# The first block of x and weights in two transfers, with roundings and products of 256 columns

## The chip, the cores and the metric

One core of one Trainium2 chip runs the whole kernel. The metric is device time in microseconds (us) of one execution; smaller is better. Before the change three runs took 620.62, 620.65 and 620.73 us (median 620.65). Beside these stands one profiled execution, with its trace.

## What is computed

A decoder trunk of two layers on 256 tokens with 1024 features, in float32. Each layer normalizes x, multiplies it by a wide input matrix (2848 columns), runs two kinds of attention on the parts, mixes them with an output matrix, and adds a squared-ReLU MLP. The part that matters here is the first product of the first layer:

```python
for l in range(DEPTH):
    h = _rms_norm(x, g_pre_mix[l])
    parts = jnp.split(h @ w_in[l], split_at, axis=-1)
    nq, kc, vc, ksel, vsel, kwin, vwin, gates, fq, fk, fv, ff = parts
    ...
    x = x + _rms_norm(mix, g_post_mix[l])
    h = _rms_norm(x, g_pre_mlp[l])
    y = jnp.square(jax.nn.relu(h @ w_up[l])) @ w_down[l]
    x = x + _rms_norm(y, g_post_mlp[l])
```

The kernel multiplies x by the gain of the norm first and scales the rows of the product by the inverse root mean square when it leaves PSUM, so the products need not wait for the norm.

## The kernel before

**Numbers.** PE multiplies in a rounded 32-bit form (`F32R`). To keep float32's accuracy every operand is split in a high half, the rounded value, and a low half, what rounding left over, and a product becomes three: high by high, high by low, low by high. `mm3` (lines 670 to 674) issues these three. So for each weight tile `wraw` there is a rounding to `whi` and a subtraction to `wlo`; for x there are `xT` high and low.

**Tiling.** Tokens are two tiles `t` of 128. The contraction over 1024 features is eight blocks `k` of 128. The input matrix is cut into column chunks (`CHUNKS`); the first that is worked on is chunk 0 of 512 columns here, in eight parts, one for each `k` (`FIRSTS`), then chunk 1 of 288 columns in four parts, and so on. `in_chunk` (lines 1060 to 1097) takes the parts in order and for each `k` and `t` calls `piece`, which issues the three products into the PSUM tile of `t`: six products of 512 columns for each `k` of chunk 0.

**The opening.** The host lays x transposed and the weights of chunk 0 side by side in one tensor, `first`: for each `k`, 256 columns of x and 512 of weights (`NFIRST` = 768), with eight columns of the gain ahead of block 0. Lines 611 to 625 load each block by one transfer on SP's queue: block 0 of 776 columns (388 KB), the others of 768. `first_xT` (lines 788 to 794) makes the two halves of x for a block, the high one on ACT and the low one on DVE, and copies the gain for block 0. `Weights.get` (lines 494 to 517) makes the two halves of a weight part: for the first two parts both on DVE, for later ones the rounding is on ACT and the subtraction on DVE. While the first block is on its way, PE runs five products of zeros (`WARM`, lines 639 to 642).

**What sets the order.** The kernel records every operation and a planner (`Recorder`, lines 184 to 408) decides the order on each engine from estimated costs, data dependencies, free buffers and due times; line 411 issues the result, so nearly all rows of the profile carry L411 and one goes by the tiles' names. `nc.after` names an operation that those recorded after it must not be planned ahead of; before the change it is set after the eighth block's transfer, and the tiles of x for the norm and the first constants follow it. Transfers take eight completion semaphores in turn, so the ninth transfer is issued only when the first has landed, the tenth when the second has, and so on.

Of the kernel before, what the change touches and what calls it, by code (L numbers as in the profile page):

```python
# [18 lines left out]
F32 = mybir.dt.float32  # L19
F32R = mybir.dt.float32r  # L20
AF = mybir.ActivationFunctionType
# [3 lines left out]
P = 128  # L25
D = 1024
S = 256
NT = 2
# [19 lines left out]
NFIRST = 768  # L48
# [433 lines left out]
class Weights:  # L482
# [11 lines left out]
    def get(self, i):  # L494
        nc, marks = self.nc, self.marks
        assert len(marks) == i
        marks.append(len(nc.ops))
        if i not in self.raw:
            nc.key = marks[max(i - LOAD_LEAD, 0)]
            self.load(i)  # L500
        kind, shape, src = self.units[i]
        raw = self.raw.pop(i)
        nc.key = None
        if kind == "raw":
            return raw
        nc.key = marks[max(i - SPLIT_LEAD, 0)]
        hi = self.tile([P] + shape, F32R, name="whi", tag="whi", bufs=WBUFS)
        lo = self.tile([P] + shape, F32R, name="wlo", tag="wlo", bufs=WBUFS)
        for j in range(shape[0]) if i < len(FIRSTS) else [slice(None)]:
            if i > 1:  # L510
                nc.scalar.activation(hi[:, j], raw[:, j], AF.Copy)
            else:

                nc.vector.tensor_copy(hi[:, j], raw[:, j])
            nc.vector.tensor_sub(lo[:, j], raw[:, j], hi[:, j].bitcast(F32))
        nc.key = None
        return hi, lo


def body(tc, A, consts_in, out):  # L520
    with ExitStack() as ctx:

        sb = {False: ctx.enter_context(tc.tile_pool(name="ops", bufs=1))}
        sb[True] = ctx.enter_context(tc.tile_pool(name="sb", bufs=1))
        pp = ctx.enter_context(tc.tile_pool(name="pp", bufs=1, space=PSUM))
        dram = ctx.enter_context(tc.tile_pool(name="dram", bufs=1, space=bass.MemoryType.DRAM))
        tc.nc.scalar.preload_act_table_set("natural_log_exp_and_others")
        rec = Recorder(tc.nc, tc)
        trunk(rec, A, consts_in, out, sb, pp, dram)
        rec.emit()  # L530


def trunk(nc, A, consts_in, out, sbp, pp, dram):
    def tile(shape, dtype, name, tag=None, bufs=1):
        return nc.tile(sbp[(tag or name) not in OPERANDS], shape, dtype, name, tag, bufs)

    def psum(tag):
        return nc.tile(pp, [P, 512], F32, tag, tag, {"acc": 2, "x": 2, "s": 3, "o": 1}[tag], psum=True)
# [20 lines left out]
    for l in range(DEPTH):  # L559
        at = 0  # L560
        for c, (a, b) in enumerate(CHUNKS):
# [3 lines left out]
            for q, (k0, k1) in enumerate(parts_of(l, c)):  # L565
# [4 lines left out]
                if (c, q) in RIDES:  # L570
                    s, j = RIDES[c, q]
# [24 lines left out]
    def weight(*key):  # L596
        return W.get(index[key])
# [13 lines left out]
    for k in range(8):  # L611
        if k in (2, 3):
            f = both[:, k - 2]
        elif k < 2:
            f = tile([P, D], F32, name="first", tag="raw", bufs=RBUFS)
        else:
            f = tile([P, D], F32, name="first", tag=f"act{k % 2}", bufs=2)
        o = 0 if k else 8
        f = f[:, 0:o + NFIRST]
        a = 8 + k * NFIRST - o  # L620
        nc.sync.dma_start(f, A["first"][:, a:a + o + NFIRST])
        if k == 0:
            gcol0 = f[:, 0:8]
        xTk.append(f[:, o:o + S])
        W.raw[k] = f[:, None, o + S:o + NFIRST]
# [14 lines left out]
    ps = psum("o")  # L640
# [29 lines left out]
    def mm3(ps, a, b, start, stop, check=True):  # L670

        for j, (u, v) in enumerate(((0, 0), (0, 1), (1, 0))):
            nc.tensor.matmul(ps, a[u], b[v], start=start and j == 0, stop=stop and j == 2,
                             skip_group_check=not check)
# [29 lines left out]
    def new_xT():  # L704
        both = tile([P, 8, 2, S], F32R, name="xT", bufs=1)
        return [both[:, :, j, :] for j in range(2)] + [both]
# [79 lines left out]
    xT = new_xT()  # L786
# [13 lines left out]
    for l in range(DEPTH):  # L800
        first = l == 0
# [105 lines left out]
        def hidden_part(s, q):  # L907
            if q == 0:
                T["w1"] = []
            T["w1"].append(weight(l, "w1" + s, q))  # L910
            if q == 3:
                T["hid"] = psum("o")
                with nc.stretch():
                    for i in range(16):
                        c = i % 4
                        nc.tensor.matmul(T["hid"][32 * c:32 * c + 32, :256],
                                         kst[s][:, i, :, :].rearrange("p g n -> p (g n)"), T["w1"][i // 4][:, c, :],
                                         start=i < 4, stop=i >= 12, tile_position=(0, 32 * c))
                    if s == "v":
                        compressed_scores()  # L920
                T["hs" + s] = tile([P, 256], F32, name="hs")
                nc.vector.tensor_copy(T["hs" + s], T["hid"][:, :256])
# [137 lines left out]
        def in_chunk(c, evac, by_token=False):  # L1060
            n = CHUNKS[c][1] - CHUNKS[c][0]
            parts = parts_of(l, c)
            begin = len(nc.ops)
            ps = [None, None]
            ws = {}

            def piece(t, k, hi, lo, k0):
                if k == 0:
                    ps[t] = psum("o" if by_token and t == 0 else "x" if c in (0, 2) else "acc")
                mm3(ps[t][:, :n], [y[:, k, t * P:t * P + P] for y in xT[:2]], (hi[:, k - k0, :], lo[:, k - k0, :]),  # L1070
                    k == 0, k == 7)

            if by_token:
                for t in range(NT):
                    for q, (k0, k1) in enumerate(parts):
                        if t == 0:
                            ws[q] = weight(l, "in", c, q)
                        for k in range(k0, k1):
                            piece(t, k, *ws[q], k0)
                            yield  # L1080
                    evac(t, ps[t])
                    yield
                return
            for q, (k0, k1) in enumerate(parts):
                w = weight(l, "in", c, q)
                for k in range(k0, k1):
                    for t in range(NT):
                        piece(t, k, *w, k0)
                        yield
                if (c, q) in RIDES:  # L1090
                    hidden_part(*RIDES[c, q])
                    yield
            nc.key = begin if EVKEY else None
            for t in range(NT):
                evac(t, ps[t])
            nc.key = None
            yield
# [78 lines left out]
        def stream():  # L1176
            def part(name, gen):
                yield from gen
                done.add(name)
            yield from part("c1", in_chunk(1, evac1))  # L1180
            yield from part("c2", in_chunk(2, evac2))
            yield from part("c3", in_chunk_T(3, "fqT"))
            yield from part("c4", in_chunk_T(4, "fkT"))
            yield from part("c5", in_chunk(5, evac5))
            for k in range(LASTK):
                while ("o", k) not in done or "nsa" not in done:
                    yield "wait"
                yield from part(("out", k), out_k(k))
# [187 lines left out]
        o = None  # L1376
        nc.lane = len(nc.ops)
        for i in range(len(flat) + 4):
# [16 lines left out]
            j = i - 3  # L1395
            if 0 <= j < len(flat) and flat[j][2] == 1 and flat[j][3] != 1:
                kind, pair, par, br = flat[j]
                if pair % 2:
                    o = psum("o")
# [3 lines left out]
                    cols = lambda q: [(q // 2) * HD] * 2 if br else [2 * q * HD, 2 * q * HD + HD]  # L1403
# [12 lines left out]
        xT = new_xT()  # L1416
# [108 lines left out]
        for fc in range(8):  # L1525
# [12 lines left out]
            if fc < 7:  # L1538
                for k in range(4):
                    w = weight(l, "dn", fc, k)  # L1540
# [6 lines left out]
            if not last_l:  # L1547
                xT = new_xT()
# [67 lines left out]
```

## Time and profile before

| | |
|---|---|
| median of 3 runs | 620.65 us (620.62 to 620.73) |
| the profiled execution's own time | 620.53 us |
| its span, first to last instruction | 618.4 us |
| PE busy | 611.0 us (99%) |
| DVE busy | 465.3 us (75%) |
| ACT busy | 388.9 us (63%) |
| moved by DMA | 118.86 MB, mean 192 GB/s |

PE is TensorE's matmul stream and PEld its loads of weights, which overlap the matmuls; DVE is VectorE, ACT ScalarE, SP the engine whose queue issues the transfers. A row of the timeline has its start in us from the span's start, its length in us (of all instructions merged in it), the engine, the line, the operation, what it writes and reads, its form, how many are merged, and in brackets how long the engine was idle before it and what ended that. The length of a matmul in the trace holds its whole passage through the array, so matmuls that follow each other overlap and the distance of their starts is what one costs. In a table of windows the columns are the window, its length, the busy time (and number of instructions) of PE, PEld, DVE, ACT and POOL, the granted clock of PE, the share of time that the DMA engines were busy, and GB/s.

### The profile page before, as it was taken

Reading aid. Unit: us, or ns where it says so; the run is one execution under the profiler, and the core shown is the slowest. Engines: PE = TensorE matmul, PEld = TensorE weight load, DVE = VectorE, ACT = ScalarE, POOL = GpSimd, SP = SyncE. Lnnn points to the kernel's source line nnn. Section 1 sums busy time; section 2 is a strip of 40 time slices with the busy share of each in tenths; the row PEclk is TensorE's granted clock in tenths of the full one; section 3 lists DMA queues with packets and bytes.
Section 4 is the critical chain, followed back from the end, with each engine's and each line's share of the span. In section 5 each row is a group of like instructions: output and inputs, shape, how many; then the busy total and the mean of one; then the engine's idle time right before and its main releaser. Section 6 shows DMA issues by size and latency. Waiting matters only on the chain.

```text
span 618.4 us, 9854 instructions
## 1 busy us (share of the span) xinstructions
PE 611.0 (99%) x3494; PEld 514.6 (83%) x3494; DVE 465.3 (75%) x1021; ACT 388.9 (63%) x760; POOL 10.8 (2%) x20
## 2 busy tenths in 40 slices
PE   9999999999999999999999999999999999999995
PEld 7989987788888888888888888778888888888884
DVE  6889998689966567557598999886996575566534
ACT  7766788567655555545466769775776456456522
POOL 0001200000000000000000020000000000000000
PEclk9999999999999999999999999999999999999998
DMA  8996746519765565564346781653386665666001
GB/s 323 401 355 209 268 137 223 171 36 307 254 191 191 182 205 196 184 197 140 107 137 239 265 312 71 204 205 104 131 299 203 191 197 175 200 197 181 32 0 68
DMA packets 34817, 118.86 MB, mean 192 GB/s; under 512 B 4144, under 2 KB 4304, under 8 KB 34768
## 3 DMA queue, kind: packets, MB, share of 16 engines
q1 hardware_dynamic: 34768, 118.23, 57.5%
q8 instruction: 27, 0.44, 0.3%
q14 instruction: 22, 0.18, 0.1%
HBM read 117.15 MB, written 1.07 MB: 191 GB/s over the span
## 4 chain that ended last, share of the span: by engine, by line
PE 99%; DVE 0%; DVEq 0%; issue 0%; ACT 0%
PE s L411 35%; PE acc L411 31%; PE x L411 25%; PE o L411 7%; DVE x L411 0%; DVE m L411 0%; DVEq L1612 0%; DVE rsqrt L411 0%; ACT rl L411 0%
## 5 line engine op out<-in xcount | busy, mean ns | idle before, releaser
L411 DVE TENSOR_TENSOR wlo<-wraw,whi 128x1024 fp32r<-128x1024 f32 (+1 forms) x188 | 225.5, 1201 | 97.9 <-ACT whi L411 57.9
L411 ACT ACTIVATE whi<-wraw 128x1024 fp32r<-128x1024 f32 (+1 forms) x188 | 195.4, 1042 | 108.2 <-PE acc L411 72.9
L411 PE MATMUL s<-xT,whi 128*128 128x512 f32 x448 | 106.5, 390 | 0.0
L411 PEld LDWEIGHTS s<-xT,whi 128*128 128x128 f32 x448 | 83.4, 188 | 16.8
L411 PE MATMUL x<-whi,aT 128*128 128x512 f32 x256 | 88.6, 391 | 0.0
L411 PE MATMUL acc<-whi,aT 128*128 128x512 f32 x256 | 88.4, 390 | 0.0
L411 PEld LDWEIGHTS s<-xT,wlo 128*128 128x128 f32 x448 | 57.4, 191 | 2.2
L411 PE MATMUL s<-xT,wlo 128*128 128x256 f32 x448 | 58.1, 283 | 0.0
L411 PEld LDWEIGHTS acc<-whi,aT 128*128 128x128 f32 x256 | 48.0, 188 | 10.0
L411 PEld LDWEIGHTS x<-whi,aT 128*128 128x128 f32 x256 | 48.1, 188 | 9.6
L411 PE MATMUL x<-wlo,aT 128*128 128x512 f32 x128 | 50.0, 390 | 0.0
L411 PE MATMUL acc<-wlo,aT 128*128 128x512 f32 x128 | 49.9, 390 | 0.0
L411 ACT ACTIVATE pr<-pr,st 128x256 f32<-128x256 f32 (+1 forms) x96 | 42.8, 449 | 5.8 <-DVE st L411 5.5
L411 PE MATMUL acc<-xT,whi 128*128 128x256 f32 (+1 forms) x192 | 42.4, 324 | 0.0
L411 PE MATMUL acc<-whi,xT 128*128 128x512 f32 (+1 forms) x128 | 37.2, 354 | 0.0
L411 PE MATMUL x<-whi,xT 128*128 128x512 f32 x112 | 35.7, 395 | 0.1
L411 PEld LDWEIGHTS acc<-xT,whi 128*128 128x128 f32 x192 | 31.7, 190 | 3.3 <-issue 0.8
L411 ACT ACTIVATE h<-s 128x256 f32<-128x256 f32 x56 | 21.2, 378 | 16.0 <-PE s L411 16.0
L411 ACT ACTIVATE rl<-h 128x512 f32<-128x512 f32 x28 | 17.7, 633 | 18.0 <-DVE h L411 18.0
L411 PE MATMUL acc<-xT,wlo 128*128 128x256 f32 x128 | 28.6, 286 | 0.0
L411 ACT ACTIVATE rl<-x 128x512 f32<-128x512 f32 x24 | 14.6, 610 | 22.2 <-PE x L411 18.0
L411 PEld LDWEIGHTS acc<-wlo,aT 128*128 128x128 f32 x128 | 24.0, 188 | 5.0
(220 smaller groups left out, 963.6 us busy)
## 6 DMA issues: line engine op xcount, KB each, us to landing
wraw<-in_w_up_dram SPq DMA_DIRECT2D x64, 512.0 KB, 4.0
wraw<-in_w_down_dram SPq DMA_DIRECT2D x64, 512.0 KB, 3.7
wraw<-in_w_in_dram SPq DMA_DIRECT2D x36, 512.0 KB, 4.9
wraw<-in_w_out_dram SPq DMA_DIRECT2D x16, 512.0 KB, 5.6
w<-in_cmp_w_k_dram SPq DMA_DIRECT2D x8, 512.0 KB, 4.9
w<-in_cmp_w_v_dram SPq DMA_DIRECT2D x8, 512.0 KB, 4.6
bias<-sums SPq DMA_DIRECT2D x8, 384.0 KB, 6.1
first<-in_first_dram SPq DMA_DIRECT2D x7, 384.0 KB, 5.2
```

The source lines that it names most:

```text
L411: getattr(getattr(self.nc, op.engine), name)(*[real(v) for v in args], **{k: real(v) for k, v in kw.items()})
```

## The change

Three edits belong together.

- Block 0 is loaded by two transfers: the gain, x and the first 256 columns of weights (520 columns), then the other 256 columns of weights. `nc.after` is set after the second of them, so that the seven other blocks stay behind both.
- Part 0 of the weights is rounded and subtracted in two halves of 256 columns, each on DVE.
- In `in_chunk`, block 0 of the first layer's chunk 0 is multiplied by column halves: both token tiles for the first 256 columns, then both for the rest, twelve products of 256 columns for six of 512. Only the first of them opens the PSUM tile's accumulation (`start`), and the group check is off, as a tile is now opened once for two column ranges.

```diff
@@ Weights.get
         for j in range(shape[0]) if i < len(FIRSTS) else [slice(None)]:
-            if i > 1:
-                nc.scalar.activation(hi[:, j], raw[:, j], AF.Copy)
-            else:
-
-                nc.vector.tensor_copy(hi[:, j], raw[:, j])
-            nc.vector.tensor_sub(lo[:, j], raw[:, j], hi[:, j].bitcast(F32))
+            for n in (slice(0, 256), slice(256, 512)) if i == 0 else [slice(None)]:
+                x, y, z = ((w[:, j, n] if i == 0 else w[:, j]) for w in (raw, hi, lo))
+                if i > 1:
+                    nc.scalar.activation(y, x, AF.Copy)
+                else:
+
+                    nc.vector.tensor_copy(y, x)
+                nc.vector.tensor_sub(z, x, y.bitcast(F32))
@@ trunk, the loads of the first blocks
-        nc.sync.dma_start(f, A["first"][:, a:a + o + NFIRST])
+        cut = o + NFIRST - 256 if k == 0 else o + NFIRST
+        for u, v in ((0, cut), (cut, o + NFIRST)):
+            if u < v:
+                nc.sync.dma_start(f[:, u:v], A["first"][:, a + u:a + v])
+        if k == 0:
+            nc.after = nc.ops[-1]
@@ in_chunk
-            def piece(t, k, hi, lo, k0):
-                if k == 0:
+            def piece(t, k, hi, lo, k0, n=slice(0, n)):
+                if k == 0 and not n.start:
                     ps[t] = psum("o" if by_token and t == 0 else "x" if c in (0, 2) else "acc")
-                mm3(ps[t][:, :n], [y[:, k, t * P:t * P + P] for y in xT[:2]], (hi[:, k - k0, :], lo[:, k - k0, :]),
-                    k == 0, k == 7)
+                mm3(ps[t][:, n], [y[:, k, t * P:t * P + P] for y in xT[:2]], (hi[:, k - k0, n], lo[:, k - k0, n]),
+                    k == 0 and not n.start, k == 7, check=False)
...
                 for k in range(k0, k1):
-                    for t in range(NT):
-                        piece(t, k, *w, k0)
-                        yield
+
+                    for cols in (slice(0, 256), slice(256, 512)) if first and c == 0 and k == 0 else [slice(0, n)]:
+                        for t in range(NT):
+                            piece(t, k, *w, k0, cols)
+                            yield
```

As the planner works on the whole program, its order moves elsewhere too: on PE some groups of products and transposes in the first layer's first three chunks change places, on SP one weight part of chunk 1 now comes ahead of the tiles of x, and ACT and DVE take the roundings and norm steps of chunk 1 in another order.

## The prediction

> **What bounds the kernel now.** I read the page first, for the span and the chain that ended last; then that chain in order of time for the opening; then the opening's timeline; then the queue of SP.
>
> ```profile
> span 618.4 us, 9854 instructions
> ...
> PE 99%; DVE 0%; DVEq 0%; issue 0%; ACT 0%
> ```
>
> PE is nearly the whole chain, so an edit pays only where it lets PE start sooner or removes a gap in its stream. The changed block is the first real work of PE:
>
> ```profile
> 4.66 0.05 issue
> 4.71 7.46 PE x L411 x30
> ```
>
> Thirty products run in these 7.46 us. What is their pace where nothing waits? Two starts of the same kind, three products apart:
>
> ```profile
> 10.43 0.62 PE L411 MATMUL x<-whi,xT 128*128 128x512 f32 x2
> ...
> 11.11 0.62 PE L411 MATMUL x<-whi,xT 128*128 128x512 f32 x2
> ```
>
> 0.68 us for three is 0.227 each. The last of the thirty starts at 4.71 + 7.46 - 0.39 = 11.78; 29 intervals took 7.07 us, where 29 x 0.227 = 6.58 would do: 0.49 us lost inside. Before them PE is idle too: the last warming product starts at 4.38 and the one before it at 4.27, so PE is free at about 4.49, 0.22 us before the first product.
>
> ```profile
> 4.27 0.39 PE L411 MATMUL o<-const-float32-0.0 128*128 128x128 f32 x2
> ...
> 4.38 0.27 PE L411 MATMUL o<-const-float32-0.0 128*128 128x128 f32 x1
> ```
>
> So 0.49 + 0.22 = 0.71 us, 0.11% of the time, is all that this part can give; 0.2% (1.24 us) is about what a measurement tells from no change. The timeline shows who makes PE wait:
>
> ```profile
> 4.14 0.43 DVE L411 CAST whi<-first 128x512 fp32r<-128x512 f32 x1 [2.97 <-DMA first<-in_first_dram]
> 4.14 0.51 ACT L411 ACTIVATE xT<-first 128x256 fp32r<-128x256 f32 x1 [2.12 <-DMA first<-in_first_dram]
> 4.48 0.16 DVE L411 COPY gcol<-first 128x8 f32<-128x8 f32 x1
> 4.60 0.69 DVE L411 TENSOR_TENSOR wlo<-first,whi 128x512 fp32r<-128x512 f32 x1
> 4.70 0.30 PEld L411 LDWEIGHTS x<-whi,xT 128*128 128x128 f32 x2 [0.23 <-ACT xT L411]
> ...
> 5.21 0.48 DVE L411 SCALAR_TENSOR_TENSOR xT<-first,xT 128x256 fp32r<-128x256 f32 x1
> 5.34 0.30 PEld L411 LDWEIGHTS x<-wlo,xT 128*128 128x128 f32 x2 [0.35 <-DVE wlo L411]
> ...
> 5.70 0.43 DVE L411 CAST whi<-first 128x512 fp32r<-128x512 f32 x1
> ...
> 5.76 0.51 ACT L411 ACTIVATE xT<-first,gcol 128x256 fp32r<-128x256 f32 x1 [1.11 <-DVE xT L411]
> 5.91 1.14 PE L411 MATMUL x<-whi,xT 128*128 128x512 f32 x4
> 6.16 0.69 DVE L411 TENSOR_TENSOR wlo<-first,whi 128x512 fp32r<-128x512 f32 x1
> 6.32 0.30 PEld L411 LDWEIGHTS x<-whi,xT 128*128 128x128 f32 x2 [0.22 <-ACT xT L411]
> ...
> 6.90 0.30 PEld L411 LDWEIGHTS x<-wlo,xT 128*128 128x128 f32 x2 [0.28 <-DVE wlo L411]
> ```
>
> Block 0 lands at 4.14, and ACT and DVE start at once. Block 1's work starts at 5.70 on DVE and 5.76 on ACT. Both are put down to DVE, which ends block 0 at 5.69; SP's queue tells another reason for the same instant:
>
> ```profile
> 0.74 3.95 SPq L411 DMA_DIRECT2D first<-in_first_dram  x8
> 4.73 0.54 SPq L411 DMA_DIRECT2D x<-in_x_dram  x1
> 5.69 0.33 SPq L411 DMA_DIRECT2D wraw<-in_w_in_dram  x1
> 6.64 0.33 SPq L411 DMA_DIRECT2D x<-in_x_dram  x1
> ...
> SPq L411 <- DMA first<-in_first_dram: 4.2, 7, 0.7
> ```
>
> Eight issues go out one behind the other; from then on each waits for a block to land, the tenth for block 1. So block 1 landed at about 5.67, and block 2 at 6.62: even if DVE were done with block 0 earlier, block 1 would not be there. This decides my forecast.
>
> **The change part by part.** *The first piece's landing.* It leaves out 128 KB of 388. At the rate of the full stream (399 GB/s below) that is 0.33 us, at the mean rate until block 0 landed (188) 0.70; the issue-to-landing latency may also not shrink at all.
>
> ```profile
> 0.74:4.12 3.38, 3.35 (x8) 2.75 (x9) 0.37 (x3) 1.27 (x1) 0.00 (x0) 1.00 0.62 188
> 7.00:9.00 2.00, 2.00 (x10) 1.66 (x10) 1.93 (x5) 2.00 (x5) 0.00 (x0) 1.00 1.03 399
> 24.00:33.00 9.00, 9.00 (x45) 7.50 (x44) 8.49 (x31) 6.42 (x17) 0.00 (x0) 1.00 1.03 403
> ```
>
> So it lands between 3.44 and 4.14; I take 3.81, since the bytes left out are the last ones, which move when the stream is nearly full.
>
> *DVE.* For block 0 two instructions of 512 columns become four of 256. The subtraction costs 0.69 at 512; at 256 columns a row of the same form has 0.42:
>
> ```profile
> L411 DVE TENSOR_TENSOR pcs<-cs,pcs 128x256 fp32r<-128x256 f32 x4 | 1.5, 420 | 0.3 <-ACT pcs L411 0.3
> ```
>
> Two are 0.15 more than one. The rounding (0.43 at 512) lies between 0.21 and 0.43 at 256; I take 0.29, as the fixed part of the subtraction (0.42 x 2 - 0.69 = 0.15) added to half of 0.43 minus that part. Two are 0.15 more. Neighbours overlap by some 0.08 (gcol starts at 4.48, the rounding ends at 4.57), twice: DVE's work for block 0 grows by 0.15 + 0.15 - 0.16 = 0.14. It took 4.14 to 5.69 = 1.55; now 3.81 + 1.69 = 5.50. The Trainium skill ("VectorE: DVE Perf Modes", section "The TRN2 errata — SBUF-src ops pay a fixed extra latency per instruction") speaks against halving: it advises tiles of at least 512 elements, and its measured fixed term of about 150 cycles would make the 256-column rounding (150 + 128)/0.96 = 290 ns, by its figures; DVE would be done at the same 5.50.
>
> *PE within block 0.* The first product may start when ACT's rounding of x is done, 3.81 + 0.51 = 4.32, but PE is behind the warming products until 4.49: 0.22 sooner than 4.71. Six products of 512 columns become twelve of 256:
>
> ```profile
> 38.74 0.40 PE L411 MATMUL acc<-xT,whi 128*128 128x256 f32 x2
> 38.98 0.28 PE L411 MATMUL acc<-xT,wlo 128*128 128x256 f32 x1
> 39.10 0.40 PE L411 MATMUL acc<-xT,whi 128*128 128x256 f32 x2
> ```
>
> 0.36 us for three: 0.12 each, so twelve take 1.44 in place of 6 x 0.227 = 1.36, and the loads of weights, twice as many, still keep up. With the waits between (the low half of x at about 5.0, the second low half of the weights at 3.81 + 1.69 + 0.1 = 5.6, then four products, and about 0.1 lost after a wait, 0.49 over the four waits of the timeline) PE is done with block 0 at about 6.3. Before, its last product started at 5.91 + 0.23 = 6.14 and ended its slot at 6.37. The 0.22 and the 0.08 both end in the wait for block 1.
>
> *Block 1.* Its bytes stand behind the same 388 KB, now in 256 rows. Lower bound of the delay: none, as the rate sets it. Upper bound: one issue slot, 3.95/8 = 0.49, since every later block is issued one slot later. The rate itself hardly falls with row size: 399 GB/s in rows of 3 KB, 403 in a stage mainly of 4 KB rows, or 16 x 3072/399 = 123 ns and 16 x 4096/403 = 163 ns per row of an engine; extrapolated to no bytes, a row costs about 5 ns, and eight more per engine 0.04. I take 0.05, near the rows: block 1 lands at 5.72. ACT's x for it, the load at 6.32 and the load at 6.90 all move by that: +0.05. From here PE uses 1.36 us a block and the stream brings one in 0.97, so a late block is not made up on PE.
>
> *SP.* Queue slots go round by eights: block 7 is now the ninth transfer and waits for the first piece (landed 3.81) when its slot comes at 0.74 + 8 x 0.49 = 4.7: no wait. What was issued ninth and on moves by one, and the planner puts a weight part of the next chunk ahead of the tiles of x. The stream stays full, so this is order, not time.
>
> *The order behind it.* In the changed program PE's order differs at a few places only; one counts: the two groups of transposes of kW and kv_tok become neighbours.
>
> ```profile
> 28.77 0.60 PE L411 MATMUL s<-cst,kW 128*128 128x128 f32 x4
> 29.13 0.48 PE L411 MATMUL x<-wlo,xT 128*128 128x512 f32 x1
> 29.45 0.39 PE L411 MATMUL x<-whi,xT 128*128 128x512 f32 x1
> 29.68 0.60 PE L411 MATMUL s<-cst,kv_tok 128*128 128x128 f32 x4
> 30.03 0.47 PE L411 MATMUL x<-whi,xT 128*128 128x512 f32 x1
> ```
>
> The product after such a group takes 0.32 (29.13 to 29.45) in place of 0.227, so one fewer leaving saves 0.09. Sum: +0.05 - 0.09 = -0.04, against a profiled execution of 620.53 us around its span of 618.4; that execution is 0.12 under the median of 620.65, so **620.6**.
>
> **The rivals.** (1) *Faster*: block 1 lands early enough that DVE sets the pace, say 5.5. Then PE runs on at 6.3 without the waits at 6.32 and 6.90, two of the four that share the 0.49: about 0.25 saved there and 0.09 later, 620.65 - 0.34 = 620.3. For it: the gap from 4.14 to 5.67 is longer than the 0.95 to the next block; against: the stream was already busy then. (2) *Slower*: the issue slot passes through whole, block 1 lands at 5.67 + 0.49 = 6.16, and PE stands for it; it decides from a landing past 5.76. 620.65 + 0.49 - 0.09 = 621.05, say 621.0. Against it: blocks are issued long before they land. The Trainium skill ("DMA: Bandwidth & Descriptors", section "Measured (HBM→SBUF, 128 partitions, SWDGE, issued from GpSimd)") leans to it, asking for transfers of 1 MiB and more; by the row above, 384 KB transfers already move at 399 GB/s when they queue, above its 341 for 1 MB. (3) *The first piece is not earlier* (4.14): DVE ends block 0 at 5.83 and holds block 1 by 0.14; 620.65 + 0.14 - 0.09 = 620.7. (4) *A stall in the next chunk*, in which ACT has no room:
>
> ```profile
> 9.00:16.00 7.00, 7.00 (x33) 5.79 (x32) 6.10 (x15) 6.92 (x18) 0.00 (x0) 1.00 1.04 392
> 16.00:20.30 4.30, 4.30 (x35) 4.26 (x34) 3.79 (x19) 4.30 (x14) 0.00 (x0) 1.00 1.04 409
> ```
>
> If a tile lands late there, all behind it in ACT's queue is late. Priced with no slack on PE: a weight part that falls back by two places in SP's queue, at 0.95 a place (5.69 to 6.64), 1.9 us: 622.5. The full stream and the unchanged bytes speak against it.
>
> **How the numbers follow.** Forecast 0.55, (1) 0.15, (2) 0.12, (3) 0.14, (4) 0.04. The range 620.2 to 621.1 takes in (1) to (3). Faster by over 0.2% needs more than the opening's 0.71 us: 0.02; slower by over 0.2% is (4) and what I don't see: 0.05; within 0.93.
>
> **What would show it.** First rounding on DVE at about 3.8, first product at 4.5, a wait at block 1's first products with its work starting at about 5.75, and PE's later stream shifted by under 0.1. A start of block 1 before 5.6 is (1), after 6.0 (2); idle PE past 12 us is (4). A first product still at 4.7 would make the account of the opening wrong.

## The result, and the profile after

| | before | after |
|---|---|---|
| median of 22 runs each, side by side | 620.76 us (620.55 to 621.36) | 621.93 us (621.47 to 622.28) |
| the profiled execution's own time | 620.53 us | 621.69 us |
| its span | 618.4 us | 619.4 us |

The ratio is 1.0018, with a 95% interval of 1.0012 to 1.0024: the changed kernel is slower by 1.17 us. That is outside the predicted range of 620.2 to 621.1.

The page of the changed kernel, its span and the engines of the chain that ended last:

```profile
span 619.4 us, 9874 instructions
...
PE 98%; DMA 1%; DVE 0%; issue 0%; SPq 0%; ACT 0%; DVEq 0%; ACTq 0%
```

A transfer is now on the chain, which it was not before. The same chain in order of time (start, length, what) shows which one. First the changed kernel's:

```profile
0.74 0.38 SPq L411
...
1.18 0.42 SPq L411
...
1.65 5.14 DMA first<-in_first_dram
...
6.88 0.52 ACT xT L411
...
7.43 9.93 PE x L411 x42
```

and of the kernel before the one stretch that holds the same products and the six ahead of them:

```profile
4.71 11.54 PE x L411 x48
```

The chain goes through the third transfer, which is block 1: issued at 1.65, landed at 1.65 + 5.14 = 6.79. Before, it was issued at 1.18 and landed at 5.67. The stretches of PE end at 4.71 + 11.54 = 16.25 and 7.43 + 9.93 = 17.36, that is 1.11 us later. The two spans are 1.0 us apart, so the opening holds the whole loss, and about 0.1 is won back behind it. (The executions' own times differ by 1.16; the rest lies outside the spans.) The opening's timeline in the changed kernel:

```profile
0.74 4.78 SPq L411 DMA_DIRECT2D first<-in_first_dram  x9
0.77 4.18 PE L411 MATMUL o<-const-float32-0.0 128*128 128x256 f32 x10 [0.77 <-PEq L1615]
...
3.96 0.29 DVE L411 CAST whi<-first 128x256 fp32r<-128x256 f32 x1 [2.79 <-DMA first<-in_first_dram]
3.96 0.51 ACT L411 ACTIVATE xT<-first 128x256 fp32r<-128x256 f32 x1 [1.95 <-DMA first<-in_first_dram]
...
4.60 0.77 PE L411 MATMUL x<-whi,xT 128*128 128x256 f32 x2
...
5.17 0.63 PE L411 MATMUL x<-wlo,xT 128*128 128x256 f32 x2
5.35 0.43 DVE L411 TENSOR_TENSOR wlo<-first,whi 128x256 fp32r<-128x256 f32 x1
...
5.60 0.93 PE L411 MATMUL x<-whi,xT 128*128 128x256 f32 x4
...
6.48 0.28 PE L411 MATMUL x<-whi,xT 128*128 128x256 f32 x1
...
6.60 0.28 PE L411 MATMUL x<-wlo,xT 128*128 128x256 f32 x1
...
6.72 0.28 PE L411 MATMUL x<-whi,xT 128*128 128x256 f32 x1
6.80 2.22 SPq L411 DMA_DIRECT2D x<-in_x_dram  x3
6.81 0.43 DVE L411 CAST whi<-first 128x512 fp32r<-128x512 f32 x1 [1.04 <-DMA first<-in_first_dram]
6.88 0.51 ACT L411 ACTIVATE xT<-first,gcol 128x256 fp32r<-128x256 f32 x1 [2.41 <-DMA first<-in_first_dram]
...
7.43 0.30 PEld L411 LDWEIGHTS x<-whi,xT 128*128 128x128 f32 x2 [0.64 <-ACT xT L411]
```

Block 0 goes well: work on its first piece starts at 3.96, its first product starts at 4.60 instead of 4.71, and DVE is done with it at 5.35 + 0.43 = 5.78. Then DVE stands for 1.04 us and ACT for 2.41, both for block 1. Its work starts at 6.81, its first load of weights at 7.43 where it was 6.32.

Why is block 1 late? The DMA traffic of the first 7 us, before and then after, and the table of windows from 4 to 7 us, before and then after (its last number is GB/s):

```profile
DMA packets 595, 1.65 MB, mean 236 GB/s; under 512 B 58, under 2 KB 58, under 8 KB 595
```

```profile
DMA packets 669, 1.46 MB, mean 209 GB/s; under 512 B 66, under 2 KB 194, under 8 KB 669
```

```profile
4.00:7.00 3.00, 2.95 (x13) 1.78 (x11) 2.82 (x7) 1.37 (x3) 0.00 (x0) 1.00 1.00 354
```

```profile
4.00:7.00 3.00, 3.00 (x16) 2.71 (x14) 1.93 (x7) 0.59 (x2) 0.00 (x0) 1.00 0.94 304
```

The stream is slower: 0.19 MB less has arrived by 7 us, about 0.5 us of the full stream (399 GB/s). The trace also has, for each transfer, the moment at which each of the 16 DMA engines was done with its part. Before, the first engine was done with block 1 at 4.88, the eighth at 5.14, the fifteenth at 5.56 and the last at 5.67. After, these were 4.57, 5.38, 6.00 and 6.79. So the first engine is earlier than before and the last is 1.12 us later: the engines have become unequal, and a block has landed only when its slowest engine is done.

### The profile page after: what moved, and what is told of

Its sections match the earlier page's. It is cut to its first block, busy times and chain, and to the rows that moved or that the text cites. A ratio compares the mean times of both kernels' runs of the same rounds, so it can differ in the third digit from the quotient of the medians.

```text
span 619.4 us, 9874 instructions
## 1 busy us (share of the span) xinstructions
PE 611.7 (99%) x3500; PEld 515.9 (83%) x3500; DVE 465.2 (75%) x1023; ACT 388.7 (63%) x760; POOL 8.4 (1%) x20
## 3 DMA queue, kind: packets, MB, share of 16 engines
HBM read 117.15 MB, written 1.07 MB: 191 GB/s over the span
## 4 chain that ended last, share of the span: by engine, by line
PE 98%; DMA 1%; DVE 0%; issue 0%; SPq 0%; ACT 0%; DVEq 0%; ACTq 0%
PE s L411 35%; PE acc L411 31%; PE x L411 25%; PE o L411 7%; DMA first<-in_first_dram 1%; SPq L411 0%; DVE x L411 0%; DVE m L411 0%; DVEq L1621 0%; ACT xT L411 0%; DVE rsqrt L411 0%; ACT rl L411 0%; ACTq L411 0%
## 5 line engine op out<-in xcount | busy, mean ns | idle before, releaser
L411 PE MATMUL x<-whi,xT 128*128 128x512 f32 (+1 forms) x116 | 36.5, 394 | 0.4 <-ACT xT L411 0.4
```

The lines of the kernel that those rows point to most:

```text
L411: getattr(getattr(self.nc, op.engine), name)(*[real(v) for v in args], **{k: real(v) for k, v in kw.items()})
```

## The experiments

The question is what in the change makes block 1 late. In the table, "issued" is the start of block 1's issue on SP's queue. "8 done" is when the eighth of the 16 DMA engines was done with it, and "landed" is when the last one was. "Starts" is the start of DVE's rounding for it, which can be later than the landing when DVE is still busy. "MB" is what DMA moved in the first 7 us. All these are from one profiled execution. The ratio is to the kernel before on the same chip, from 5 to 11 runs (22 for the change), with its 95% interval.

| run | issued | 8 done | landed | starts | MB | ratio |
|---|---|---|---|---|---|---|
| the kernel before | 1.18 | 5.14 | 5.67 | 5.70 | 1.65 | |
| the change | 1.65 | 5.38 | 6.79 | 6.81 | 1.46 | 1.0018 (1.0012 to 1.0024) |
| e1 only the two transfers | 1.66 | 5.40 | 6.69 | 6.71 | 1.43 | 1.0026 (1.0015 to 1.0037) |
| e2 only the halved roundings and products | 1.18 | 5.10 | 5.57 | 5.88 | 1.68 | 1.0004 (0.9995 to 1.0013) |
| e3 two transfers of 64 partitions | 1.99 | 5.67 | 7.06 | 7.08 | 1.28 | 1.0031 (1.0019 to 1.0042) |
| e4 two transfers, cut between x and weights | 1.65 | 5.81 | 7.45 | 7.47 | 1.29 | 1.0024 (1.0015 to 1.0033) |
| e10 three pieces | 2.11 | 5.60 | 6.74 | 6.76 | 1.40 | 1.0024 (1.0015 to 1.0033) |
| e5 the change, block 4 and later held | 1.65 | 5.40 | 7.32 | 7.34 | 1.30 | 1.0023 (1.0014 to 1.0032) |
| e6 the kernel before, block 4 and later held | 1.18 | 4.99 | 5.59 | 5.95 | 1.62 | 1.0009 (1.0000 to 1.0019) |
| e7 the change, block 2 and later held | 1.65 | 4.94 | 5.51 | 5.79 | 1.08 | 1.0032 (1.0018 to 1.0047) |
| e11 the change, block 2 held a little | 1.65 | 4.81 | 6.03 | 6.05 | 1.38 | 1.0025 (1.0014 to 1.0035) |
| e8 block 4 in two transfers instead | 1.17 | 5.69 | 6.43 | 6.45 | 1.43 | 1.0005 (0.9995 to 1.0014) |
| e9 the change, second piece on ACT's queue | 1.17 | 5.05 | 5.60 | 5.62 | 1.68 | 1.0004 (0.9995 to 1.0013) |
| e12 the kernel before, with a small transfer more | 1.66 | 5.15 | 6.75 | 6.78 | 1.38 | 1.0016 (1.0007 to 1.0025) |

### Which half of the change: e1 and e2

e1 is the kernel before with the diff's loop of `cut` in the loads alone; e2 is the kernel before with the diff's edits of `Weights.get` and `in_chunk` alone.

> Block 0 in two transfers as in the change; its roundings and products stay at 512 columns, so all work on the weights of block 0 waits for the second piece. Theory A (more and shorter rows at the head of the stream slow it, so block 1 lands about 1.1 us late whatever is computed): DVE starts block 1 at about 6.7 to 6.9 us, time 621.7 to 622.0. Theory B (one more issue slot, 0.49 us): block 1 starts at 6.2, time 621.2. Theory C (the halved work, or the earlier work on DVE, ACT and PE, disturbs the stream): block 1 starts at 5.7, time 620.7.

> Block 0 in one transfer as before; roundings and products of block 0 in halves of 256 columns. Theories A and B (the transfer is the cause): block 1 lands at about 5.7 and DVE, with 0.14 us more work, starts it at 5.8: time 620.7 to 620.9. Theory C: block 1 starts at 6.5 or later, time over 621.5.

The halves cost nothing that can be told; the transfers make block 1 late. In e1:

```profile
5.56 1.19 PE L411 MATMUL x<-whi,xT 128*128 128x512 f32 x2 [0.61 <-DVE whi L411]
...
6.55 0.63 PE L411 MATMUL x<-wlo,xT 128*128 128x512 f32 x1
...
6.71 0.43 DVE L411 CAST whi<-first 128x512 fp32r<-128x512 f32 x1 [0.57 <-DMA first<-in_first_dram]
...
6.98 0.63 PE L411 MATMUL x<-whi,xT 128*128 128x512 f32 x1
...
7.41 0.63 PE L411 MATMUL x<-wlo,xT 128*128 128x512 f32 x1
```

Block 1 is late as in the change, 6.71. That e1 lost more than the change (622.59 against 620.72 us, 1.87) has a cause of its own in the profiled execution: the planner put x's low half ahead of the weights' rounding on DVE, so the first product came at 5.56 only, and products then came 0.43 us apart (6.55, 6.98, 7.41; see the last section). So its landing is to be read here, not its ratio. In e2 block 0 comes whole and a little late in that execution, 4.41; block 1 follows on time, as SP's wait for it ends at 5.59, ahead of DVE:

```profile
5.59 0.33 SPq L411 DMA_DIRECT2D wraw<-in_w_in_dram  x1
...
5.88 0.42 DVE L411 CAST whi<-first 128x512 fp32r<-128x512 f32 x1
```

### What of the transfer: e3, e4 and e10

More rows, shorter rows, or the mere transfer? e3 cuts block 0 by partitions, so that rows stay 3104 bytes and their number 128:

```diff
+        for u in (0, 64) if k == 0 else (None,):
+            r = slice(None) if u is None else slice(u, u + 64)
+            nc.sync.dma_start(f[r], A["first"][r, a:a + o + NFIRST])
+        if k == 0:
+            nc.after = nc.ops[-1]
```

> Block 0 in two transfers by partitions, 64 rows of 3104 bytes each, 128 rows in all as before; roundings and products as before. Theory A (number and length of rows): block 1 starts at about 5.7 as before, time 620.7. Theory B (one more transfer and slot ahead): block 1 starts at 6.2 or later, time 621.2 or more.

e4 cuts between x and the weights (`cut = o + S`); the planner put the weights' piece first.

> Block 0 in two transfers, cut between x and the weights (rows of 1056 and 2048 bytes), roundings and products as before. Theory A: as many rows as in the change, so block 1 starts at 6.7 to 6.9 and the time is 621.7 to 622.0. Theory B: 6.2 and 621.2. If what matters is that the second piece's rows are only 1 KB, block 1 starts at about 6 and the time is about 621.

e10 loads block 0 in three transfers: 264, 256 and 256 columns.

```diff
-        for u, v in ((0, cut), (cut, o + NFIRST)):
+        for u, v in ((0, o + S), (o + S, cut), (cut, o + NFIRST)) if k == 0 else ((0, cut),):
             if u < v:
                 nc.sync.dma_start(f[:, u:v], A["first"][:, a + u:a + v])
+                nc.after = nc.ops[-1] if k == 0 else nc.after
```

> Block 0 in three transfers (gain and x; 256 columns of weights; 256 columns of weights), computing as in the change. Theories S and H: a second additional transfer at the head costs about as much again as the first: block 1 starts at 7.3 to 8, time 622.6 to 623.2. If only having a piece at all matters (a one-off disturbance), block 1 stays at 6.8 and the time at 621.9.

All three are slower. In e3 and e4 block 0's second piece is late too (ACT's first work is at 5.26 and 5.06), so again it is block 1's start that tells. e3, with neither a row more nor a shorter one, has it at 7.08. (Its two issues took longer, 0.57 and 0.58 us in place of 0.38 and 0.42, so block 1 was issued at 1.99.) So neither more rows nor shorter ones are needed for the delay. In e10 the two additional pieces cost block 1 no more than one did: it starts at 6.76, where twice the price would give about 7.9. So it is not a fixed price for each transfer that adds up. In e10 the two issue slots alone account for 0.93 of the 1.07 us by which block 1 lands later than before.

### What goes on behind block 1: e5, e6, e7, e11 and e8

Here later transfers are held back. In e5 (on the change) and e6 (on the kernel before) GpSimd copies a column of block 0 into block 4's tile, which block 4 then overwrites, so blocks 4 to 7 are issued only once block 0's first transfer has landed. The edit also keeps the later weight loads behind block 7, in lines that are left out here. e7 does the same with `k == 2`. In e11 three fills with zeros of block 2's tile hold it until 3.08 only.

```diff
+        if k == 4:
+            nc.gpsimd.tensor_copy(f[:, 0:1], gcol0[:, 0:1])
...
+        if k == 4:
+            nc.after = nc.ops[-1]
```

> The change, and SP's queue held at block 4: GpSimd writes one column of block 4's tile from block 0's gain, so block 4 and all behind it are issued only once the first piece has landed (about 4.3 us). Theory F (the rows of block 1 are slow because issuing further transfers, the seventh to ninth, disturbs the ones under way: SP's issues grow from 0.43 to 0.6-0.7 us at the same time as the slow rows): block 1 starts at 5.3 to 5.8, time 620.4 to 620.8. Theory G (an additional transfer at the head costs by itself, whatever is issued behind): block 1 starts at 6.7 to 6.9, time 621.7 to 622.0.

> The kernel before, with the same hold at block 4. Theory F: block 1 starts somewhat earlier than 5.7 (5.2 to 5.6), time 620.4 to 620.7. Theory G: nothing changes, block 1 at 5.7, time 620.7. If the hold itself costs (later blocks late), PE waits past 8 us and the time is over 621.

> The change, held already at block 2, so only the two pieces and block 1 are in flight until the first piece has landed. Theory F: block 1 starts at 4.9 to 5.4; block 2 follows its own issue (4.3) by at least 2 us. Theory G: block 1 still at 6.7 or later.

> The change, with block 2 and all behind it held on SP until GpSimd has filled block 2's tile three times with zeros (estimate: until about 3 us, in place of 2.1), with no wait for a landing. Block 1 then has the queue to itself for some 0.9 us more. Theory S with transfers prepared side by side (block 1's rows wait since blocks 2 and 3 are prepared at the same time): block 1 starts at 5.5 to 5.9, block 2 soon enough, time 620.3 to 620.9. Theory H: block 1 at 6.5 or later, time 621.7 or more.

In e5 nothing is issued from 3.0 to 4.35, and block 1 starts at 7.34 all the same. In e6 the same hold without the additional transfer leaves block 1's landing on time, at 5.59. The hold itself isn't free: e6's median is 621.51 where the kernel before has 620.65 (its profiled run, at 622.04, is the slowest of its ten), and there ACT waits 1.62 us for block 4. So the ratios of the held versions hold the price of the hold too, and only their landings are to be read. In e7 only the two pieces and block 1 are under way until 4.42, and block 1 lands at 5.51 in spite of the piece ahead; then block 2 is late. As issuing goes on at 4.35 in e5 and at 4.42 in e7, both while block 1 is in flight, that isn't what delays it. e7's timeline, and its chain:

```profile
5.60 0.51 ACT L411 ACTIVATE xT<-first,gcol 128x256 fp32r<-128x256 f32 x1 [1.03 <-DMA first<-in_first_dram]
...
5.79 0.42 DVE L411 CAST whi<-first 128x512 fp32r<-128x512 f32 x1
```

```profile
4.42 4.00 DMA first<-in_first_dram
...
9.53 8.46 PE x L411 x36
```

So the delay takes both in these traces: the additional transfer ahead, and transfers behind it that were issued before 3 us (blocks 2 and 3 in e5, none in e7). That the additional transfer alone costs nothing isn't shown, as no run holds block 2 in the kernel before. e11 lies between: block 1 starts at 6.05, and block 2 pays (it lands at 8.25, in the change at 7.73). e7 and e11 are one profiled execution each.

e8 puts the cut in block 4 (`k == 4` in place of `k == 0`), five places behind.

> The kernel before, with block 4 in two transfers (512 and 256 columns) in place of block 0; block 0 whole, all computing as before. If an additional transfer harms only when it stands at the head, ahead of block 1, block 1 starts at 5.7 and the time is 620.7. If what harms is the number of transfers issued early in all, block 1 starts at 6.2 or later and the time is over 621.2.

Its median cannot be told from before. Its profiled run, the slowest of its ten at 621.41, has block 1 at 6.45 and 1.43 MB: a late block 1 can come without a piece ahead of it, too, but by the median not in the usual run. No profile here counts how often it comes in which kernel, so the claims below rest on the medians where there are any.

### Which queue, and how small: e9 and e12

e9 issues the second piece on ACT's queue; SP issues the first piece and then block 1. The edit also gives the planner a cost for transfers on ACT's queue, in lines that are left out here.

```diff
-                nc.sync.dma_start(f[:, u:v], A["first"][:, a + u:a + v])
-        if k == 0:
-            nc.after = nc.ops[-1]
+                (nc.scalar if u else nc.sync).dma_start(f[:, u:v], A["first"][:, a + u:a + v])
```

> The change, with the second piece of block 0 issued from ACT's queue (after its table load, at about 2.0 us) in place of SP's, so block 1 is again SP's second transfer. Theory S (SP's transfers are prepared one after the other at a cost per transfer that small pieces do not hide, so block 1 comes late by what one more transfer takes there): block 1 starts at 5.6 to 5.9, time 620.4 to 620.8. Theory H (any additional transfer in flight at the head upsets the stream, whichever queue it is on): block 1 starts at 6.5 or later, time over 621.5.

e12 is the kernel before with 16 KB more between block 0 and block 1, into a tile that nothing reads:

```diff
         nc.sync.dma_start(f, A["first"][:, a:a + o + NFIRST])
+        if k == 0:
+            nc.after = nc.ops[-1]
+            extra = small([P, 32], "extra", 1)
+            nc.sync.dma_start(extra, A["first"][:, 8:40])
+            nc.after = nc.ops[-1]
```

> The kernel before, with one more transfer on SP's queue between block 0 and block 1: 32 columns (16 KB, rows of 128 bytes) into a tile that nothing reads. It adds no work on any other engine, and no block is cut. Theory S (what costs is one more transfer ahead of block 1 in SP's queue, whatever it carries): block 0 lands about as before (4.0 to 4.3 us), block 1's work starts at 6.4 to 6.9 instead of 5.70, ratio 1.001 to 1.003. Rival B (the bytes or the cut block are what costs: 16 KB are 0.04 us of the full stream): block 1 starts at 5.7 to 5.85, ratio within 0.999 to 1.0008. A start between 6.0 and 6.3 would say that only the issue slot of 0.49 us passes through.

e9's opening, the windows row and the traffic:

```profile
0.74 3.90 SPq L411 DMA_DIRECT2D first<-in_first_dram  x8
...
0.76 0.39 ACTq L411 DMA_DIRECT2D first<-in_first_dram  x1
...
4.04 0.49 DVE L411 CAST whi<-first 128x256 fp32r<-128x256 f32 x2 [2.87 <-DMA first<-in_first_dram]
...
5.62 0.43 DVE L411 CAST whi<-first 128x512 fp32r<-128x512 f32 x1
```

```profile
4.00:7.00 3.00, 3.00 (x17) 2.91 (x16) 2.94 (x9) 1.34 (x3) 0.00 (x0) 1.00 1.01 365
```

e12's opening and its windows row:

```profile
1.19 0.42 SPq L411 DMA_DIRECT2D extra<-in_first_dram  x1
1.66 4.23 SPq L411 DMA_DIRECT2D first<-in_first_dram  x7
4.08 0.51 ACT L411 ACTIVATE xT<-first 128x256 fp32r<-128x256 f32 x1 [2.07 <-DMA first<-in_first_dram]
...
6.78 0.43 DVE L411 CAST whi<-first 128x512 fp32r<-128x512 f32 x1 [1.14 <-DMA first<-in_first_dram]
```

```profile
4.00:7.00 3.00, 3.00 (x10) 2.33 (x8) 1.77 (x5) 0.67 (x2) 0.00 (x0) 1.00 0.92 274
```

With the same bytes, the same cut and the same computing, but the piece on the other queue, the loss is gone: 365 GB/s in place of 304, block 1 at 5.62. ACT issued the piece at 0.76, not at about 2.0 as expected, so all of block 0 was issued in e9 ahead of block 1, as in the change. And 16 KB that cut nothing and serve nothing bring the loss back whole: block 1 at 6.78, ratio 1.0016. In e12 eight engines are done with block 1 at 5.15, as before (5.14), and only the slower ones are late. So what costs is one more transfer ahead of block 1 on SP's queue, and neither its bytes nor its use.

One thing these runs don't separate: a transfer more on SP's queue also puts block 1's issue one slot later (1.65 for 1.18), and no run moves that issue without a transfer. The late issue alone isn't enough, as e7 has it and lands on time; and 0.47 us of issue is less than half of the 1.1.

The Trainium skill ("DMA: Bandwidth & Descriptors", section "Issuing engines are not separate DMA queues") says that starting transfers from several engines saves only the time that the sequencer needs to start them. Here that time is the slot of 0.42 us in e12's row, and block 1's start moved by 1.2 (6.81 to 5.62) between the queues; the measurement decides.

No version ran faster than the kernel before. e9 had block 1 on time and its first product at 4.61, and still gained nothing that can be told. Its chain shows PE without a gap, but the stretch ends at 4.95 + 11.71 = 16.66, 0.41 later than before, as PE went through most of block 0 at half its pace in that execution (last section):

```profile
4.95 11.71 PE x L411 x54
```

## Why the prediction was wrong

- **Block 1, "I take 0.05": this step failed.** The delay measured 1.1 (5.67 to 6.79). The upper bound failed too, not only the value: "Upper bound: one issue slot, 3.95/8 = 0.49" took the delay of issuing for the most that a transfer can cost those behind it. The issue did move by about that, 0.47 (1.18 to 1.65). But the stream from 4 to 7 us then ran at 304 GB/s in place of 354, and its engines were done with block 1 over 2.22 us in place of 0.79. The trace of before holds no case of one more transfer in that place, so its rows bounded only the delay of issuing.
- **Rival (2) had place and sign right** (its mark was a start of block 1 after 6.0) and its price at under half. Its sum was 620.65 + 0.49 - 0.09 = 621.05. With 1.11 in place of the slot, without the 0.09, and from the median of the 22 runs of before, it would be 620.76 + 1.11 = 621.87, where 621.93 was measured.
- **The argument against it was the wrong one**: "blocks are issued long before they land" is true of both kernels. Block 1 was issued 4.5 us ahead of landing before and 5.1 us ahead after.
- **The first piece**: 3.81 predicted, work starts at 3.96, within the bounds. **First product**: 4.49 predicted, 4.60 measured, as the last two warming products started 0.21 apart here, where it was 0.11 before (last section).
- **DVE**: a rounding of 256 columns took 0.29 and a subtraction 0.43, as estimated; done with block 0 at 5.78 rather than 5.50, from the later landing (0.15) and neighbours that overlap less. It waited for block 1 after that.
- **PE within block 0** was mis-sized too, and it didn't show. The forecast had twelve products in 1.44, and with the waits PE done at about 6.3. They ran from 4.60 to 6.72 + 0.12 = 6.84: the first took 0.36, six followed 0.21 apart (5.17 to 5.60 for two), and the last five took 0.12 each. With block 1 late, PE still waited by its weight loads' row (0.64), so it cost nothing here. In e9, where block 1 was on time, it did cost (16.66 for 16.25).
- **That the gain at the first product would "end in the wait for block 1"** held: the 0.11 us gained there went into that wait.
- **SP, "order, not time"**, and no stall in the next chunk (rival 4): held. From the first product of block 1 on, both kernels are 1.11 us apart and stay so up to the end of chunk 0. The 0.09 of the transposes did not come: behind them, at the chain's next stretch of products (30.27 before, 31.40 after), the kernels are 1.13 apart. The 0.1 by which the spans close on each other came later.
- **What is shown and what is open.** Shown by medians and traces: the loss comes with one more transfer ahead of block 1 on SP's queue (e12, with e1, e3, e4 and e10 alike in their landings), and without it the loss is gone (e2, e9). Shown by one trace each: it takes transfers close behind (e5 with e6, and e7). Refuted as causes: the halved computing and the bytes, number and length of rows. Open: what in the queue makes the engines unequal and the stream slow from 4 to 7 us, as no profile here shows inside it, and whether the transfer itself does it or the later issue of block 1 with a stream close behind.

## What to carry to other kernels

Don't price one more transfer at the head of a full queue by its bytes or by its issue slot. Measure it, and read the GB/s of the windows just behind it: 16 KB cost here as much as 128. Where a first piece must come sooner, try to issue what is split off on a queue that is otherwise idle; here that took the loss away (e9) but brought no gain. Count first what the piece's consumer waits for next: if it is the following block, an earlier start is worth nothing. An upper bound taken from the one cost that the profile of before shows is a bound on that cost alone.

## What had not been expected of the hardware

PE changes to its full pace at a moment that differs from one execution to the next. In the profiled execution of before, the zero products reached it at about 4.3 us. After, the products above are 0.21 apart until 6.2 and 0.12 from there. And in e1, where PE stood for 0.61 us ahead of its first product, products of 512 columns came 0.43 apart up to 10.0, and 0.23 from there. In the 14 profiles the change lay between 3.7 and 10.0 us. The column of the granted clock says 1.00 in all these windows, so one reads it from the distance of the starts. The Trainium skill ("TensorE: Matmul & The Clock Gate", section "What's actually happening") describes this: half the clock until a busy window of 3.4 us has passed, with windows that don't begin with the kernel. The traces agree on the half pace and on the varying moment. The length of the window they don't bear out: in e6 the full pace came at 3.7, 2.9 us behind PE's first product at 0.77. One profiled execution thus shows one draw of the opening, and costs read at 0.227 us for a product hold only behind that moment.
